# A hybrid decoder block on one core: the loads of branch A's blocks move from SyncE's DMA queue to POOL's

## The chip, the cores and the metric

The kernel runs on one core of one Trainium2 chip. The metric is the device time of one execution in microseconds (us); the time given is the median of several executions. One further execution was recorded by the hardware profiler; its span and its trace are what the rows below come from.

The engines are named as in the profile: PE (TensorE, matmuls), DVE (VectorE), ACT (ScalarE), POOL (GpSimd) and SP (SyncE, which here only issues DMAs). A name with a q behind it (SPq, POOLq) is the engine's sequencer, which issues DMAs and waits for semaphores.

## The reference, cut to what matters

```python
def reference(x, p, w_in, ..., w_branch_a, w_branch_b, w_out, ...):
    h = rms_norm(x, g_pre)
    proj = h @ w_in                                   # 1024 x 1024 @ 1024 x 9216
    u, v, z_a, q, f, inp, z_b, a_a, a_b = split(proj)
    y_a = gmlp_spatial_gating(gelu(u), gelu(v), ...)
    y_a = (y_a * silu(z_a)) @ w_branch_a              # branch A
    o = hgrn2_chunked(q_h, k_in, log_f, v_h)
    o = rms_norm(o, hgrn_norm_g)
    y_b = (o * silu(z_b)) @ w_branch_b                # branch B
    merged = sigmoid(a_a) * y_a + sigmoid(a_b) * y_b
    x = x + rms_norm(merged @ w_out, g_post)
    e = p @ w_ple
    gate = sigmoid(x @ w_ple_gate + b_ple_gate)
    return x + rms_norm(e * gate, g_ple)
```

Sequence and width are 1024, everything is float32. The change lies at the seam between the last columns of `proj` (`a_b`, called AB here) and the product with `w_branch_a`.

## The kernel before

Every large matmul is done with operands split into a high and a low part (`hi`, `lo`): three matmuls stand for one. The split of a tile is a cast on ACT (L134) and a subtraction on DVE (L135). The products of `w_in`, `w_branch_a` and `w_out` are done in two-by-two blocks with seven block products instead of eight (`pair`, whose sums of weight blocks are the tiles `S` and `S2`, made on DVE at L789, and whose results are put together at L812 in tiles `k`, five buffers). A block product is 12 matmuls of 128x512.

The weights of a pair come in two loads of 512 KB with rows of 1 KB (`half_load`, L862). In the main part they land in tiles `raw`; in the stretch looked at here two pairs run in turns (`both`), one with results in the PSUM tiles `big` and one in `small`, and their four loads land in tiles `raw2` (four buffers; the profile prints `raw` for both, the order of instructions keeps them apart by name and number).

What branch A multiplies is computed earlier, block by block, by `mix_a`, and stored to DRAM as seven blocks `af_b11, af_b21, af_b22, af_t1 ... af_t4`. Before the product with `w_branch_a` they are loaded back: the loop at L1002 calls `fill` seven times, `fill` makes two loads of 512 KB each into tiles `raw` (`RAWS` = 3 buffers, rows of 4 KB) and splits them into `a_b11h`, `a_b11l` and so on. These fourteen loads are issued at L891. `fill` is also called at four other places (branch B's blocks, `w_out`, the gate), on which nothing changes here.

The order of instructions on each engine is set by a scheduler when the kernel is built; each engine then runs its own in that order, so an instruction that waits holds everything behind it on that engine. SP issues nearly all loads. POOL issues the stores of intermediate results: `stored` (L905, tiles `k` to `gb_sp` and others), L932 (`bf_sp`) and L766 (`b_sp`, a head's output). Names that the steps below use: `raw2_9424, raw2_9426, raw2_9428, raw2_9430` are the four loads for the pairs AB2 and AB3; `raw2_9753` to `raw2_9769` are the first four of `w_branch_a`; `q<-b_sp7` is the reload (L901) of the last head's output, which POOL stores at L766; `k_9383` is the result at L812 that reads the PSUM bank which the last block product of the projection before AB2 goes on writing.

Of the kernel before, what the change touches and what calls it, by code (L numbers as in the profile page):

```python
# [16 lines left out]
P = 128  # L17
# [16 lines left out]
def hybrid_block(  # L34
# [22 lines left out]
    nc = tc.nc  # L57
    x, p, w_in, out = x[0], p[0, 0], w_in[0], out[0]
# [21 lines left out]
    af_sp = {n: dram.tile([P, 4, 512], F32, name=f"af_{n}") for n in ("b11", "b21", "b22", "t1", "t2", "t3", "t4")}  # L80
# [52 lines left out]
    def split(hi, lo, src):  # L133
        nc.scalar.copy(out=hi, in_=src)  # L134
        nc.vector.tensor_tensor(out=lo, in0=src, in1=hi.bitcast(F32), op=ALU.subtract)  # L135
# [53 lines left out]
    def wide_load(w, kh, c0, pl=None, tag="raw"):  # L189
        raw = (pl or wp).tile([P, 4, 256], F32, tag=tag, name=tag, bufs=RAWS)  # L190
        nc.sync.dma_start(out=raw, in_=w[kh * 512:(kh + 1) * 512, c0:c0 + 256].rearrange("(k p) c -> p k c", p=P))
        return raw
# [21 lines left out]
    def slot(pl, tag, shape, name):  # L214

        return [pl.tile(shape, F32R, tag=f"{tag}{n}", name=f"{name}{n}") for n in "hl"]
# [23 lines left out]
    for tp in range(4):  # L240
        nc.sync.dma_start(out=pins[:, 2 * tp:2 * tp + 2, :],
                          in_=p[tp * 256:(tp + 1) * 256, :].rearrange("(t p) c -> p t c", p=P))
        if tp % 3 == 0:
            s = slice(tp // 3 * 512, tp // 3 * 512 + 512)
            raw = wp.tile([P, 2, 512], F32, tag="raw", name="raw", bufs=RAWS)
# [29 lines left out]
    for quarter in range(4):  # L275
# [5 lines left out]
        if quarter < 2:  # L281
            raw = wide_load(w_in, quarter, COL_I)
# [10 lines left out]
        for kp in range(NK // 2):  # L293
# [4 lines left out]
            for i in range(2):  # L298
                k = 2 * kp + i
                hi, lo = (a(k, q0, 256) for a in hT)  # L300
                src = pt[:, i * 256:(i + 1) * 256]
# [31 lines left out]
    def folded(n, w, name):  # L333

        return kp.tile([P, 4 * n, w], F32, tag=f"{name}m", name=f"{name}m"), kp.tile([P, n, w], F32, tag=f"{name}f", name=f"{name}f")

    def fold(m, f, dst):
# [3 lines left out]
        for k in (2, 3):  # L341
# [3 lines left out]
    m, f = folded(16, 1, "sub")  # L345
    nc.gpsimd.memset(m, 1.0)
    nc.gpsimd.affine_select(out=m, in_=m, pattern=[[-2, 64], [0, 1]], compare_op=ALU.is_equal,
                            fill=0.0, base=0, channel_multiplier=1)
# [6 lines left out]
    for H in (2, 8):  # L355
        ns = 32 // H
        for d in (1, 2, 3):
            m, f = folded(ns // 4, (4 - d) * H, f"q{d}")
# [188 lines left out]
    for g in range(4):  # L547
# [3 lines left out]
                            fill=0.0, base=0, channel_multiplier=-1)  # L551
# [330 lines left out]
    def at(tag):  # L882
        return (xp if tag[0] == "x" else xq), tag

    def fill(tag, src, shape, name):

        b = slot(*at(tag), shape, name)
        n = shape[1] // 2
        for k in (0, n):
            raw = wp.tile([P, n, shape[2]], F32, tag="raw", name="raw", bufs=RAWS)  # L890
            nc.sync.dma_start(out=raw, in_=src[:, k:k + n, :])  # L891
            split(*(a[:, k:k + n, :] for a in b), raw)
        return b

# [105 lines left out]
    a_blocks = {}  # L1000
    wa = loads_of_two(row_parity(w_branch_a), 0)
    for n, tag in (("b11", "x00"), ("t4", "x01"), ("t2", "t1"), ("t1", "t0"), ("t3", "t2"), ("b21", "x10"), ("b22", "x11")):  # L1002
        a_blocks[n] = fill(tag, af_sp[n], [P, 4, 512], f"a_{n}")
        if n in ("t1", "t3"):
            r = next(wa)

# [20 lines left out]

    first = weight_load(cols(w_branch_b, 0, 0))
    B = [fill(tag, bf_sp[k], [P, 2, T], f"B{k}") for k, tag in enumerate(("x00", "x01", "t1", "t0"))]
    wo = row_halves(w_out)  # L1030
    o_blocks = {}
# [4 lines left out]
    for j in range(8):  # L1036
        py = dense_tile()
        w = weight_split(first, split)
        for parts in ((((0, 512),), ((512, 512),)) if j == 7 else (((0, 512), (512, 512)),)):
            accumulate(py, w, (B_part(0), B_part(1)), parts)  # L1040
        if j < 7:
            first = weight_load(cols(w_branch_b, 0, j + 1))
        if j < 3:
            n, tag = (("b11", "t2"), ("t4", "x10"), ("t2", "x11"))[j]
            o_blocks[n] = fill(tag, wo_sp[n] if j else wo[0][:, :, 0:512], [P, 4, 512], f"wo_{n}")
        for half in range(2):
            q = reload(gb_sp[j], half)
            nc.vector.tensor_tensor(out=q, in0=py[half], in1=q, op=ALU.mult)
            nc.vector.tensor_tensor(out=merged(j, half), in0=pairs_of(q), in1=pairs_of(reload(ma_sp[j], half)), op=ALU.add)
# [136 lines left out]
```

## Time and profile before

| | us |
|---|---|
| median of 3 runs | 1241.37 |
| lowest and highest of them | 1239.43, 1244.89 |
| the profiled execution, whole | 1236.92 |
| its span in the trace | 1235.2 |
| PE busy in the span | 1205.0 |
| DVE busy | 875.1 |
| ACT busy | 599.9 |
| POOL busy | 167.6 |

A row of a timeline gives start, duration, engine, line, operation, output<-input, count, and in brackets the idle time of the engine ahead of it with what ended it. In the chain of work that ended last each row is a start, a duration and what the time was spent in. Times are us from the start of the span.

### The profile page before, as it was taken

To read this page: it belongs to the slowest core of one execution; us is meant where nothing else is said; L and a number is where in the kernel's file an instruction comes from. 1 tells how busy PE (TensorE), PEld (TensorE's weight loads), DVE (VectorE), ACT (ScalarE), POOL (GpSimd) and SP (SyncE) were. 2 spreads that over 40 slices of the span, in tenths; PEclk is the share of its full clock that TensorE was granted. 3 is DMA by queue.
4 is the path that set the end of the run, shared out by engine and by line. 5 is a ranking of instruction groups with operands and counts; after the bars stand their busy time and mean duration, and the time that the engine had idled before them with its cause. 6 is when DMAs were issued, how large, how long until landed. Compare 5 with 4: busy or idle time off the path is not lost.

```text
span 1235.2 us, 22089 instructions
## 1 busy us (share of the span) xinstructions
PE 1205.0 (98%) x8536; PEld 1015.4 (82%) x8536; DVE 875.1 (71%) x1747; ACT 599.9 (49%) x1049; POOL 167.6 (14%) x303
## 2 busy tenths in 40 slices
PE   9999999999999999999999999999999999999996
PEld 6999999778887787888878788887788788787886
DVE  5986665567675967687785857756765644988876
ACT  7642433646556456456555545535724321545332
POOL 4136721010100101010101100100110000000000
PEclk9999989999999999999999999999999999999999
DMA  8636622434535446234533433347853874515232
GB/s 302 202 120 222 203 108 95 132 127 136 166 118 170 156 151 211 95 134 149 187 130 111 167 116 120 109 148 235 283 197 129 285 226 145 171 46 177 86 103 69
DMA packets 111978, 192.58 MB, mean 156 GB/s; under 512 B 8920, under 2 KB 68352, under 8 KB 111872
## 3 DMA queue, kind: packets, MB, share of 16 engines
q1 hardware_dynamic: 93904, 132.42, 33.7%
q0 software_dynamic: 17968, 58.74, 13.1%
q8 instruction: 67, 1.10, 0.4%
q14 instruction: 39, 0.32, 0.1%
HBM read 128.48 MB, written 62.65 MB: 155 GB/s over the span
## 4 chain that ended last, share of the span: by engine, by line
PE 54%; issue 25%; DVE 9%; DMA 5%; ACT 3%; POOL 3%; SPq 1%; DVEq 0%; POOLq 0%; ACTq 0%
PE big L785 25%; PE big L169 6%; PE small L785 2%; PE big L206 2%; PE big L207 2%; PE big L205 2%; PE big L1119 2%; PE big L1121 2%; PE big L1120 2%; PE small L109 1%; DMA raw<-in_w_in_dram 1%; DVE lo L135 1%; PE small L206 1%; PE small L207 1%; PE small L205 1%
## 5 line engine op out<-in xcount | busy, mean ns | idle before, releaser
L135 DVE TENSOR_TENSOR lo<-S,hi 128x512 fp32r<-128x512 f32 x168 | 118.0, 705 | 88.1 <-ACT hi L134 87.9
L134 ACT CAST hi<-S 128x512 fp32r<-128x512 f32 x168 | 103.4, 618 | 149.5 <-PE big L785 81.2
L134 ACT CAST hi<-raw 128x512 fp32r<-128x512 f32 x126 | 77.2, 618 | 139.9 <-PE big L785 63.5
L135 DVE TENSOR_TENSOR lo<-raw,hi 128x512 fp32r<-128x512 f32 x126 | 85.7, 687 | 71.5 <-ACT hi L134 69.1
L812 DVE TENSOR_TENSOR k<-big,k 128x512 f32<-128x512 f32 x90 | 61.8, 687 | 16.5 <-PE big L785 12.1
L789 DVE TENSOR_TENSOR S<-raw 128x512 f32<-128x512 f32 x58 | 39.9, 688 | 22.8 <-DMA raw<-in_w_in_dram 19.9
L785 PE MATMUL big<-h11l,hi 128*128 128x512 f32 x108 | 44.4, 411 | 2.3 <-DVE k L812 2.3
L785 PE MATMUL big<-t1l,hi 128*128 128x512 f32 x108 | 43.7, 404 | 2.0 <-ACT hi L134 2.0
L785 PE MATMUL big<-t1h,lo 128*128 128x512 f32 x108 | 43.3, 401 | 1.0 <-DVE lo L135 1.0
L785 PE MATMUL big<-t2l,hi 128*128 128x512 f32 x108 | 43.3, 401 | 0.4 <-ACT k L807 0.4
L785 PE MATMUL big<-t3l,hi 128*128 128x512 f32 x108 | 43.7, 404 | 0.0
L785 PE MATMUL big<-t0l,hi 128*128 128x512 f32 x108 | 43.5, 403 | 0.0
L785 PE MATMUL big<-h00l,hi 128*128 128x512 f32 x108 | 43.3, 401 | 0.0
L785 PE MATMUL big<-h10l,hi 128*128 128x512 f32 x108 | 43.1, 399 | 0.0
L785 PE MATMUL big<-t1h,hi 128*128 128x512 f32 x108 | 43.1, 399 | 0.0
L785 PE MATMUL big<-h11h,lo 128*128 128x512 f32 x108 | 43.0, 398 | 0.0
L785 PE MATMUL big<-h11h,hi 128*128 128x512 f32 x108 | 42.8, 397 | 0.0
L785 PE MATMUL big<-t0h,lo 128*128 128x512 f32 x108 | 42.7, 395 | 0.0
L785 PE MATMUL big<-h10h,lo 128*128 128x512 f32 x108 | 42.6, 394 | 0.0
L785 PE MATMUL big<-t3h,lo 128*128 128x512 f32 x108 | 42.6, 394 | 0.0
L785 PE MATMUL big<-t2h,lo 128*128 128x512 f32 x108 | 42.5, 394 | 0.0
L785 PE MATMUL big<-h00h,lo 128*128 128x512 f32 x108 | 42.5, 393 | 0.0
(670 smaller groups left out, 3834.4 us busy)
## 6 DMA issues: line engine op xcount, KB each, us to landing
raw<-in_w_in_dram SPq DMA_DIRECT2D x66, 512.0 KB, 4.4
xt<-in_x_dram SPq DMA_DIRECT2D x8, 512.0 KB, 7.4
e_sp<-ev SPq DMA_DIRECT2D x8, 512.0 KB, 4.4
v_sp<-tq POOLq DMA_DIRECT2D x32, 128.0 KB, 2.9
wo_t<-t POOLq DMA_DIRECT2D x16, 256.0 KB, 3.5
vn_sp<-tq POOLq DMA_DIRECT2D x16, 256.0 KB, 2.8
q<-vn_sp SPq DMA_DIRECT2D x16, 256.0 KB, 5.9
f_sp<-k POOLq DMA_DIRECT2D x16, 256.0 KB, 2.5
```

What stands on the lines that cost most here:

```text
L134: nc.scalar.copy(out=hi, in_=src)
L135: nc.vector.tensor_tensor(out=lo, in0=src, in1=hi.bitcast(F32), op=ALU.subtract)
L169: nc.tensor.matmul(out=ps[c0 // 512][:, c0 % 512:c0 % 512 + n], lhsT=wt(k), rhs=a(k, c0, n), start=(k == 0 and i == 0), stop=(k == NK - 1 ...
L205: nc.tensor.matmul(out=o, lhsT=al, rhs=hi, start=first, stop=False, **kw)
L206: nc.tensor.matmul(out=o, lhsT=ah, rhs=lo, start=False, stop=False, **kw)
L207: nc.tensor.matmul(out=o, lhsT=ah, rhs=hi, start=False, stop=last, **kw)
L785: nc.tensor.matmul(out=o, lhsT=w[:, k, :], rhs=x_[:, k, :], start=(k == 0 and i == 0 and not onto), stop=(k == 3 and i == 2), skip_group_c ...
L789: nc.vector.tensor_tensor(out=o, in0=x_, in1=y, op=op)
L812: nc.vector.tensor_tensor(out=o, in0=x_, in1=y, op=ALU.add)
L1119: nc.tensor.matmul(out=o, lhsT=parts[:, 1, k, :], rhs=wh, start=(k == 0), stop=False)
L1120: nc.tensor.matmul(out=o, lhsT=parts[:, 0, k, :], rhs=wl, start=False, stop=False)
L1121: nc.tensor.matmul(out=o, lhsT=parts[:, 0, k, :], rhs=wh, start=False, stop=(k == NK - 1))
```

## The change

`fill` gets an argument that names the engine whose queue issues its loads, SyncE's where none is given. The loop of branch A's seven blocks gives POOL's.

```diff
-    def fill(tag, src, shape, name):
+    def fill(tag, src, shape, name, queue=nc.sync):
...
-            nc.sync.dma_start(out=raw, in_=src[:, k:k + n, :])
+            queue.dma_start(out=raw, in_=src[:, k:k + n, :])
...
-        a_blocks[n] = fill(tag, af_sp[n], [P, 4, 512], f"a_{n}")
+        a_blocks[n] = fill(tag, af_sp[n], [P, 4, 512], f"a_{n}", nc.gpsimd)
```

Fourteen DMA issues leave SP and stand on POOL. PE's instructions keep their order. On SP, in the stretch in which the last projections run (`q_9386` is the reload of the last head's output):

```order
 L862 DMA raw_9268<-in_w_in_dram 128x4x256
 L862 DMA raw_9270<-in_w_in_dram 128x4x256
-L891 DMA raw_9715<-af_b11_125 128x1024
-L891 DMA raw_9719<-af_b11_125 128x1024
 L901 DMA q_9386<-b_sp7_76 128x512
 L901 DMA q_9392<-b_sp6_75 128x512
```

Two loads that stood ahead of the reloads, and so ahead of the loads `raw2_9424` to `raw2_9430` that follow them, are gone from SP. On POOL at the same place (the store of the last head's output, then the stores of branch B's last block):

```order
 L766 DMA b_sp7_76<-z_9260 128x1024
 L905 DMA gb_sp2_152<-k_9127 128x512
+L891 DMA raw_9719<-af_b11_125 128x1024
+L891 DMA raw_9725<-af_t4_131 128x1024
 L932 DMA bf_sp3_88<-k_9383 128x512
 L932 DMA bf_sp3_88<-k_9390 128x512
 L932 DMA bf_sp3_88<-k_9364 128x512
 L932 DMA bf_sp3_88<-k_9329 128x512
+L891 DMA raw_9729<-af_t4_131 128x1024
+L891 DMA raw_9735<-af_t2_129 128x1024
```

Two loads now stand behind the store of the head and ahead of four stores, and `raw_9725`, which on SP stood behind all four `raw2` loads, has nothing of SP's ahead of it. On DVE the scheduler writes another order at the start of AB2 and AB3 (`S` are sums of the four `raw2` loads, `lo` the low part of one):

```order
 L789 TENSOR_TENSOR S_9475<-raw2_9424,raw2_9428 128x512
 L789 TENSOR_TENSOR S2_9511<-S_9475,raw2_9424 128x512
+L789 TENSOR_TENSOR S_9493<-raw2_9426,raw2_9430 128x512
+L789 TENSOR_TENSOR S2_9531<-S_9493,raw2_9426 128x512
+L812 TENSOR_TENSOR k_9383<-big_9274,k_9364 128x512
 L135 TENSOR_TENSOR lo_9458<-raw2_9426,hi_9457 128x512
-L812 TENSOR_TENSOR k_9383<-big_9274,k_9364 128x512
-L789 TENSOR_TENSOR S_9493<-raw2_9426,raw2_9430 128x512
 L812 TENSOR_TENSOR k_9364<-big_9273,k_9364 128x512
-L789 TENSOR_TENSOR S2_9531<-S_9493,raw2_9426 128x512
```

`k_9383` stood behind three instructions that need the first three `raw2` loads; it now stands behind four of which one needs the fourth load.

## Rows read from the trace of the kernel before

**Rows 1.** The page: span, and PE's busy time, share of span, instructions.

```profile
span 1235.2 us, 22089 instructions
PE 1205.0 (98%) x8536; PEld 1015.4 (82%) x8536; DVE 875.1 (71%) x1747; ACT 599.9 (49%) x1049; POOL 167.6 (14%) x303
```

**Rows 2.** PE's waits from 790 to 960: total, times, longest (us).

```profile
PE big L785 <- DVE k L812: 2.3, 1, 2.3
PE big L785 <- DVE lo L135: 1.0, 1, 1.0
```

**Rows 3.** The chain that ended last, 824 to 843: start, duration, what.

```profile
825.31 0.34 SPq L891
...
825.70 0.43 SPq L901
...
829.30 9.95 DMA raw<-in_w_in_dram
...
841.28 0.70 DVE k L812
```

**Rows 4.** SP's waits from 780 to 960: total, times, longest (us).

```profile
SPq L891 <- DVE S L789: 18.5, 1, 18.5
...
SPq L891 <- DVE a_t3l L135: 10.6, 2, 8.7
```

**Rows 5.** Timeline of POOL, 740 to 960.

```profile
822.51 0.54 POOL L766 DMA_DIRECT2D b_sp<-z  x1 [0.60 <-ACT z L765]
824.88 0.54 POOL L905 DMA_DIRECT2D gb_sp<-k  x1 [1.83 <-ACT k L921]
844.66 1.74 POOL L932 DMA_DIRECT2D bf_sp<-k  x3 [19.24 <-DVE k L931]
...
889.28 0.54 POOL L905 DMA_DIRECT2D gb_sp<-k  x1 [4.72 <-ACT k L921]
```

**Rows 6.** DMA issues, last us to landing: at 822, at 874, whole span.

```profile
b_sp<-z POOLq DMA_DIRECT2D x1, 512.0 KB, 3.0
...
gb_sp<-k POOLq DMA_DIRECT2D x1, 256.0 KB, 7.0
...
gb_sp<-k POOLq DMA_DIRECT2D x16, 256.0 KB, 2.7
```

**Rows 7.** Timeline of DVE, 829 to 843.

```profile
829.20 0.69 DVE L135 TENSOR_TENSOR lo<-raw,hi 128x512 fp32r<-128x512 f32 x1 [2.06 <-ACT hi L134]
...
839.35 0.69 DVE L789 TENSOR_TENSOR S<-raw,raw 128x512 f32<-128x512 f32 x1 [2.80 <-DMA raw<-in_w_in_dram]
840.07 0.69 DVE L789 TENSOR_TENSOR S<-S,raw 128x512 f32<-128x512 f32 x1
840.68 0.69 DVE L135 TENSOR_TENSOR lo<-raw,hi 128x512 fp32r<-128x512 f32 x1
...
841.88 0.68 DVE L789 TENSOR_TENSOR S<-raw,raw 128x512 f32<-128x512 f32 x1
```

**Rows 8.** Three stretches: length, busy by engine, then PEclk, DMA share, GB/s.

```profile
833.00:835.00 2.00, 2.00 (x11) 1.63 (x10) 0.00 (x0) 0.00 (x0) 0.00 (x0) 1.00 1.09 371
842.00:845.20 3.20, 3.18 (x8) 2.50 (x9) 3.20 (x6) 2.25 (x4) 0.54 (x1) 0.50 0.03 12
217.00:219.00 2.00, 2.00 (x6) 1.49 (x6) 2.00 (x4) 0.94 (x3) 0.00 (x0) 0.57 0.29 87
```

**Rows 9.** The chain that ended last, 863 to 890.

```profile
870.63 6.90 DMA raw<-in_w_branch_a_dram
```

**Rows 10.** Timeline of PE: its stalls at 216, 842 and 886, a product at 900.

```profile
216.79 0.50 PE L785 MATMUL big<-t1l,hi 128*128 128x512 f32 x1 [2.02 <-ACT hi L134]
...
842.02 0.80 PE L785 MATMUL big<-h11l,hi 128*128 128x512 f32 x1 [2.35 <-DVE k L812]
...
886.51 0.50 PE L785 MATMUL big<-a_b11h,lo 128*128 128x512 f32 x1 [1.03 <-DVE lo L135]
...
899.90 0.39 PE L785 MATMUL small<-a_t2l,hi 128*128 128x512 f32 x1
```

## The prediction

> **What bounds the kernel now.** First the busy times [rows 1]: PE is busy in 1205.0 of 1235.2 us, so a change that leaves PE's own work as it is can only give back, or add to, PE's idle time, 30 us over the whole span. The change touches the stretch from the last projections to the end of branch A, so the next view is who made PE wait there [rows 2]: two stalls between 790 and 960, 2.3 us behind a result on DVE (call it stall A) and 1.0 us behind a low part on DVE (stall B). Nothing else in that stretch stops PE. Last, the chain of work at each stall, read backwards.
>
> Stall A [rows 3, 10]: PE goes on at 842.02, after 2.35 us, when DVE has finished `k_9383`, started at 841.28. DVE was late because it runs in order and had stood 2.80 us waiting for a load [rows 7]: the third `raw2` load, in flight for 9.95 us from 829.30. That was issued so late because SP came to it late: SP had waited 18.5 us, its longest wait in the stretch, for a `raw` buffer [rows 4], until a sum on DVE freed it; at 825.31 it issued the second load of `af_b11`, from 825.70 on four reloads, and then the `raw2` loads. At first sight this is what the change cures: that wait is on a load that now leaves SP.
>
> The stall costs more than its length. From 842.0 to 845.2 PE ran at a granted clock of 0.50, the 1.2 GHz level [rows 8], so 3.2 us hold the work of 1.6. Stall A costs 2.35 + 1.6 = 3.95 us. Stall B [rows 9, 10], 1.03 us ahead of 886.51, is the end of an unbroken row of DVE work that begins where a branch A weight load lands (in flight 6.90 us from 870.63); no lower clock follows it. So at most 3.95 + 1.03 = 5.0 us can be gained here, 0.4% of 1236.92.
>
> **The change part by part.** *The issues themselves.* Fourteen issues of 0.34 us [rows 3] leave SP, 4.8 us, and fourteen of 0.54 [rows 5] come to POOL, 7.6 us. Neither is on PE's path: SP waits in this stretch rather than works, and POOL sits idle 19.24 us ahead of its stores of 844.66 [rows 5]. Value 0; if POOL's idle time were gone it would be the 7.6.
>
> *SP's wait.* Behind the two removed loads the next instruction on SP is the reload of the last head's output. It needs POOL's store of that output, issued at 822.51 [rows 5] and landed 3.0 us later [rows 6], at 825.5. The reload went out at 825.70. So one wait of SP takes the place of the other and 0.2 us is gained, not 18. The store itself is not late on POOL: the load put ahead of it is the one that SP had issued before its wait of 18.5 us began, so near 806, long before POOL has a store to issue.
>
> *DVE's new order.* `k_9383` now stands behind two sums of the fourth load instead of one low part. From the starts [rows 7] a sum that follows its own input costs a step of 0.72 us, another instruction one of 0.61. Before: 0.72 + 0.61 + 0.60 = 1.93 from the first sum to `k_9383`; now 0.72 + 0.61 + 0.72 + 0.61 = 2.66. That is +0.7 us on stall A, with nothing to hide it. In addition the fourth load must be there 1.2 us earlier than where DVE used it (at 840.68 instead of 841.88, [rows 7]); the trace only shows that it had landed by 841.88. Bounds 0 and 1.2; I take 0.2, because in the order before its issue was held up behind the landing of a load that is no longer on SP.
>
> *Company on the DMA engines at stall A.* On SP the load `raw_9725` stood behind the four `raw2` loads. On POOL it goes out as soon as its buffer is free, which is after the low part of 829.20 [rows 7], so near 830, while they are in flight. The engines were full then: share 1.09 at 371 GB/s [rows 8]. Its 0.524 MB take 0.524 / 371 = 1.4 us of them. Ends: 0 (POOL's transfer gets only what SP's leaves) and +1.4 (it goes ahead of the third load whole). What the trace shows of a POOL transfer beside full engines is a 256 KB store that took 7.0 us where the median is 2.7 [rows 6]: POOL's side is the one that suffered, so I take half, 0.7. The Trainium skill, page "DMA: Bandwidth & Descriptors", section "Queues, rings and completion order", says that each DMA engine takes its queues in turn, a packet at a time; rows of 4 KB against rows of 1 KB would then put the moved load ahead and the value at +1.4; the 7.0 us store speaks against so good a share for POOL.
>
> Stall A together: −0.2 + 0.7 + 0.2 + 0.7 = +1.4 us; ends −0.2 + 0.7 = +0.5 and −0.2 + 0.7 + 1.2 + 1.4 = +3.1. The clock loss stays as it is, since the stall was already long enough for it.
>
> *Stall B.* The rest of the moved loads wait for a `raw` buffer (DVE's `a_t3l` and its like, [rows 4]), not for SP, so they go out when they did. But the two weight loads of about 870 now share the engines with the next two moved loads, which on SP stood behind them. Ends: the two pass in front whole, 2 x 1.4 = +2.8 us; or the weights, no longer behind an earlier moved load in SP's own queue, land sooner and the 1.03 us vanish. I take +0.5. A stall of 2.02 us was followed by a clock of 0.57 [rows 8, 10] and that of 1.03 by none, so if B passes 2 us some 1.6 us come on top.
>
> *Loads that now stand behind stores.* The last moved load stands behind a store that went out at 889.28 [rows 5]. The store waits for ACT, which before waited there for a moved load itself, so it will go out sooner; even at 889.28, with 0.54 us to issue and 6.90 in flight [rows 9], the load would be there near 897, 3 us ahead of the product at 899.90 [rows 10] that needs what stands behind it on ACT. Value 0; without that cover it would be up to a few us on the second pair of branch A.
>
> Sum against the profiled execution: 1236.92 + 1.4 + 0.5 = 1238.8. That execution was 4.45 us faster than the median of the runs; on the median, 1241.37 + 1.9 = **1243.3 us**.
>
> **The rivals.**
> *SP is set free* (faster). The `raw2` loads land 2.5 us or more sooner and stall A is gone with its clock loss: −3.95, so 1237.4. For it speaks the 18.5 us wait, the largest of SP's. Against it: the reload behind it is bound by a store that POOL issues at 822.51, change or not. It decides from a third load that lands before 837.
>
> *POOL's loads pass SP's weight loads* (slower). Where the engines are full, the loads from POOL's queue go in front. Stall A takes its upper end, +3.1; stall B +2.8 and, being over 2 us, +1.6 of clock: +7.5, so 1248.9. For it: the engines at 371 GB/s with share 1.09. Against it: the store of 7.0 us. It decides from where B passes 2 us.
>
> *Nothing moves.* The moved loads are bound by buffers, the reload by the store, and SP's issue time was never short; DVE's new order is made up by a fourth load that lands sooner and by less queueing at B. 1241.4. The Trainium skill, same page, section "Issuing engines are not separate DMA queues", says that issuing from another engine only saves the sequencer's issue time, here the 4.8 us of SP that lie beside waits: this case. By that sentence the time is unchanged; the trace agrees in that SP's time goes to waits [rows 4], but not in DVE's order, which the sentence does not cover.
>
> **How the numbers follow.** Forecast (+0.5 to +3.5 us) 0.50; nothing moves 0.25; SP set free 0.12; loads pass 0.13. The measurement can tell about 0.5%, 6.2 us, from no change. At most 5.0 us can be gained, so faster by over 0.5% needs the scatter of the runs too (they lie 5.5 us apart): 0.03. Slower by over 0.5% is most of the last rival: 0.10. The rest, 0.87, lies within. The range reaches down to the rival that sets SP free, 1237.5, and up past the one in which the loads pass, 1250: it leaves out about half of the first and the tail of the second.
>
> **What would show it.** The reloads on SP still go out at about 825.5 and the `raw2` loads behind them: if they go out 10 us sooner the store was not what bound them. PE's wait for `k` at L812 is 3 to 4.5 us (2.35 before), with the fourth load ahead of it on DVE; under 2 us means SP was set free. PE's wait for a low part at the start of branch A is 0.5 to 2 us; over 2 us with a clock near 0.5 behind it is the slower rival. The loads at L891 on POOL start within a microsecond of the times at which SP issued them, except the third, about 2 us sooner. The forecast is wrong if PE waits at a new place, above all behind an ACT cast of a moved load.

## The result, and the profile after

The changed kernel took 1244.4 us (median of 20 runs, 1237.14 to 1250.78). The kernel before, run again beside it, took 1237.41 us (median of 20, 1233.6 to 1244.89). The ratio is 1.0052, 95% interval 1.0036 to 1.0068: the change makes the kernel slower by about 6.4 us (0.0052 of 1237.41), at the 0.5% that the prediction called the least it could tell from no change. The two medians lie 7.0 us apart; what follows goes by the ratio.

The forecast was +1.9 us, to 1243.3. So 1244.4 lies beside the number written down, but that is luck, two errors that cancel: the three runs shown of before lay about 4 us above the later median, and the effect came out about 4.5 us larger than forecast. The sign and the places of the loss hold, the size doesn't.

The profiled execution of the change is its longest run (1250.78 us). The head of its page, to be set beside [rows 1]:

```profile
span 1249.1 us, 22099 instructions
PE 1216.8 (97%) x8536; PEld 1026.6 (82%) x8536; DVE 879.7 (70%) x1747; ACT 600.1 (48%) x1049; POOL 172.8 (14%) x317
```

PE has the same 8536 instructions and is busy 11.8 us longer; most of that lies ahead of the changed stretch (see the section on scatter), the rest is about what the lower clock behind the two stalls adds, since matmuls at a lower clock count as busy. PE's waits from 815 to 1000 us (total, times, longest):

```profile
PE big L785 <- DVE k L812: 4.4, 2, 4.1
PE big L785 <- DVE lo L135: 1.5, 1, 1.5
PE big L169 <- DVE B3l L135: 0.7, 1, 0.7
PE big L785 <- ACT hi L134: 0.3, 1, 0.3
```

The same two stalls as in [rows 2], both longer; the second, short wait for `k` and the one at L169 lie past 970 us, behind the stretch. In the timeline of PE (start, length, idle time ahead and what ended it):

```profile
851.43 0.79 PE L785 MATMUL big<-h11l,hi 128*128 128x512 f32 x1 [4.09 <-DVE k L812]
...
895.79 0.50 PE L785 MATMUL big<-a_b11l,hi 128*128 128x512 f32 x1 [0.33 <-ACT hi L134]
...
898.00 0.80 PE L785 MATMUL big<-a_b11h,lo 128*128 128x512 f32 x1 [1.48 <-DVE lo L135]
```

Stall A went from 2.35 [rows 10] to 4.09 us, stall B from 1.03 to 0.33 + 1.48 = 1.81 us.

**Stall A, read backwards.** DVE ahead of it, to be set beside [rows 7]:

```profile
847.96 0.69 DVE L789 TENSOR_TENSOR S<-raw,raw 128x512 f32<-128x512 f32 x1 [1.63 <-DMA raw<-in_w_in_dram]
848.69 0.69 DVE L789 TENSOR_TENSOR S<-S,raw 128x512 f32<-128x512 f32 x1
849.35 0.69 DVE L789 TENSOR_TENSOR S<-raw,raw 128x512 f32<-128x512 f32 x1
850.08 0.69 DVE L789 TENSOR_TENSOR S<-S,raw 128x512 f32<-128x512 f32 x1
850.69 0.68 DVE L812 TENSOR_TENSOR k<-big,k 128x512 f32<-128x512 f32 x1
```

From the first sum to `k_9383` it is now 850.69 - 847.96 = 2.73 us, 1.93 before: DVE's new order costs 0.80. The rest is the load. Two traces are laid over each other at the first product of ZB3, which starts at 823.03 in before and at 830.69 here; PE has no stall from there to stall A. The first sum then comes at 847.96 - 830.69 = 17.27, where it came at 839.35 - 823.03 = 16.32: 0.95 later. 0.95 + 0.80 = 1.75 is the growth of the stall, 4.09 - 2.35 = 1.74.

The DMA issues of this stretch (queue, count, KB each, median us from issue to landing); first before, 825 to 833.8, then the change, 828 to 840:

```profile
raw<-in_w_in_dram SPq DMA_DIRECT2D x4, 512.0 KB, 10.1
raw<-af_t SPq DMA_DIRECT2D x1, 512.0 KB, 9.9
```

```profile
raw<-in_w_in_dram SPq DMA_DIRECT2D x4, 512.0 KB, 9.5
raw<-af_t POOLq DMA_DIRECT2D x1, 512.0 KB, 6.8
```

The first load of `t4` took 9.9 us on SP's queue, behind the four `raw2` loads; on POOL's, issued while they were being issued, it took 6.8 us. It gets through sooner, and the load that DVE waits for comes later. While this load was in flight in the change (837.84 to 844.66) the two queues moved (packets, MB, share of the 16 engines; q1 is SP's queue, q0 POOL's):

```profile
q1 hardware_dynamic: 1600, 1.92, 79.2%
q0 software_dynamic: 177, 0.61, 23.6%
```

POOL's queue got about a quarter of what the engines moved. But the third load needs until near 847.9, so the whole of `t4`'s load was moved before it landed.

**The clock.** One-us windows of the change (busy time by engine, then PEclk, DMA share, GB/s); before had 0.50 for 3.2 us [rows 8]:

```profile
851.43:852.43 1.00, 1.00 (x2) 0.83 (x3) 1.00 (x2) 1.00 (x2) 0.00 (x0) 0.50 0.00 0
...
855.43:856.43 1.00, 1.00 (x4) 0.80 (x3) 0.00 (x0) 0.00 (x0) 0.00 (x0) 0.50 1.01 387
856.43:857.43 1.00, 1.00 (x5) 0.81 (x4) 0.48 (x1) 0.62 (x1) 0.00 (x0) 0.75 0.88 303
...
898.00:899.00 1.00, 1.00 (x2) 0.84 (x3) 1.00 (x2) 1.00 (x3) 0.70 (x2) 0.50 0.90 176
...
901.00:902.00 1.00, 1.00 (x5) 0.78 (x5) 0.48 (x1) 0.94 (x1) 0.25 (x1) 0.84 0.90 225
```

Five windows at 0.50, the 1.2 GHz level, and one at 0.75 follow stall A: 5 x 0.5 + 0.25 = 2.75 us lost, some 2.7 with rounded edges, where before lost 1.6. And stall B, which no lower clock followed before, now has three windows at 0.50 and one at 0.84 behind it, some 1.6 us.

**Stall B.** The chain that ended last has the weight load of [rows 9] again, and ahead of it a moved load:

```profile
871.30 6.37 DMA raw<-af_t
877.67 0.02 issue
877.69 1.06 ACT a_t2h L134
...
881.23 7.72 DMA raw<-in_w_branch_a_dram
```

The weight load is 7.72 us in flight (6.90 before). It is issued 7.91 us after the first `t0` product of AB2, 7.75 before, since its buffer and DVE's row ahead of it hang on the load of `t2`. Two of the moved loads that on SP stood behind it, the second of `t3` and the first of `b21`, go out on POOL while it is in flight:

```profile
882.63 0.53 POOL L891 DMA_DIRECT2D raw<-af_t  x1 [1.81 <-DVE a_t1l L135]
883.99 0.53 POOL L891 DMA_DIRECT2D raw<-af_b  x1 [0.83 <-DVE a_t1l L135]
```

In this pair of traces the change's loss is then: stall A +1.74 and about 1 us of clock, stall B +0.78 and 1.6 of clock, 5.1 in all. Measured over the stretches themselves, which the next section defines (26.12 to 28.90 us at A, 26.04 to 28.61 at B), it is 2.78 + 2.57 = 5.35.

### The profile page after: what moved, and what is told of

Its sections match the earlier page's. It is cut to its first block, busy times and chain, and to the rows that moved or that the text cites. A ratio compares the mean times of both kernels' runs of the same rounds, so it can differ in the third digit from the quotient of the medians.

```text
span 1249.1 us, 22099 instructions
## 1 busy us (share of the span) xinstructions
PE 1216.8 (97%) x8536; PEld 1026.6 (82%) x8536; DVE 879.7 (70%) x1747; ACT 600.1 (48%) x1049; POOL 172.8 (14%) x317
## 4 chain that ended last, share of the span: by engine, by line
issue 45%; PE 39%; POOL 5%; DVE 4%; DMA 3%; ACT 2%; POOLq 0%; DVEq 0%; SPq 0%; ACTq 0%
PE big L785 10%; PE big L169 6%; PE big L207 3%; PE big L206 3%; PE big L205 3%; PE big L1119 2%; PE big L1121 2%; PE big L1120 2%; PE small L785 2%; PE small L207 1%; PE small L206 1%; PE small L205 1%; DMA raw<-bf_sp 1%; PE small L109 1%; DMA raw<-in_w_out_dram 1%
## 5 line engine op out<-in xcount | busy, mean ns | idle before, releaser
L135 DVE TENSOR_TENSOR lo<-S,hi 128x512 fp32r<-128x512 f32 x168 | 122.3, 730 | 91.9 <-ACT hi L134 91.7
L135 DVE TENSOR_TENSOR lo<-raw,hi 128x512 fp32r<-128x512 f32 x126 | 88.7, 712 | 74.9 <-ACT hi L134 72.6
L785 PE MATMUL big<-h10h,hi 128*128 128x512 f32 x108 | 42.6, 394 | 0.0
```

Source lines behind the costliest of these rows:

```text
L785: nc.tensor.matmul(out=o, lhsT=w[:, k, :], rhs=x_[:, k, :], start=(k == 0 and i == 0 and not onto), stop=(k == 3 and i == 2), skip_group_c ...
```

## The experiments

One trace of each kernel gives four numbers beside the ratio: stall A and the length of the stretch around it (length A: from the first product of ZB3, the projection before AB2, to the first product in the bank set `small`, which is AB3's), and the same for B (from AB2's first `t0` product to the first `a_b11` product in `small`, in branch A). The lengths hold the clock's part. All in us; "by traces" is length A - 24.53 plus length B - 25.73, which are the means of the kernels that leave that part as it was (A: before, before again, e3, e5, e6; B: before, before again, e1; with e2, e7 and e9, which also leave B's loads on SP, the mean of B would be 25.9).

| kernel | stall A | length A | stall B | length B | by traces | ratio, interval |
|---|---|---|---|---|---|---|
| before | 2.35 | 26.12 | 1.03 | 26.04 | | |
| before again, e11 | 1.48 | 23.75 | 0.56 | 25.57 | | |
| the change | 4.09 | 28.90 | 1.81 | 28.61 | +7.3 | 1.0052 (1.0036 to 1.0068) |
| the change, e8 | 3.83 | 27.69 | 2.23 | 27.51 | +4.9 | |
| the change, e12 | 3.98 | 29.04 | 2.46 | 29.10 | +7.9 | |
| e1, b11 | 2.72 | 24.97 | 0.57 | 25.57 | +0.3 | 1.0013 (0.9995 to 1.0032) |
| e2, b11 and t4 | 4.26 | 28.96 | 0 | 24.96 | +3.7 | 1.0023 (1.0008 to 1.0039) |
| e3, the other five | 0.99 | 23.26 | 1.98 | 27.26 | +0.3 | 1.0027 (1.0007 to 1.0047) |
| e4, change and weights | 4.13 | 27.96 | 1.89 | 27.17 | +4.9 | 1.0039 (1.0024 to 1.0055) |
| e5, t2 and t1 | 1.04 | 23.29 | 0.94 | 25.94 | -1.0 | 1.0023 (1.0003 to 1.0043) |
| e6, t3, b21, b22 | 2.36 | 26.22 | 1.47 | 26.76 | +2.7 | 1.0021 (1.0003 to 1.0040) |
| e7, b11 and reloads | 4.29 | 29.02 | 1.47 | 26.62 | +5.4 | 1.0047 (1.0021 to 1.0073) |
| e9, sums on POOL | 0 | 21.98 | 1.48 | 26.49 | -1.8 | 0.9988 (0.9971 to 1.0005) |
| e10, change, sums on POOL | 0.71 | 22.97 | 2.06 | 27.35 | +0.1 | 1.0022 (1.0000 to 1.0044) |

The lengths of the two groups do not overlap. Where b11 and t4 are on POOL with DVE's sums left in place (the change, e2, e4) length A is 27.69 to 29.04, in the five traces that leave A alone 23.26 to 26.22. Where t3 and b21 are on POOL (the change, e3, e4, e6, e10) length B is 26.76 to 29.10, in all others 24.96 to 26.62.

### Parts of the change: e1 to e3, e5, e6

Each moves some of the seven blocks and leaves the others on SP; e2, e3, e5 and e6 differ from e1 in the names of the blocks alone.

```diff
-        a_blocks[n] = fill(tag, af_sp[n], [P, 4, 512], f"a_{n}")
+        a_blocks[n] = fill(tag, af_sp[n], [P, 4, 512], f"a_{n}", nc.gpsimd if n == "b11" else nc.sync)
```

**e1, the two loads of b11.**

> Only the two loads of block b11 are issued from POOL, the other twelve from SP as before. DVE has the order of the changed kernel at stall A (four sums ahead of the result that PE waits for), but the first load of t4 stands behind the raw2 loads on SP again, and stall B's loads are as before. Theory (the loss is DVE's order and a load from another queue beside the weights' loads, each followed by a lower clock): stall A about 2.35 + 0.8 = 3.2 us, stall B near 1.0 with no lower clock behind it, so +1 to +2 us, ratio 1.001. Rival 1 (DVE's order does not matter, all of it is the shared engines): stall A 2.3, within 0.5 us of before. Rival 2 (the loss lies outside the stretch, or comes with any change of the program): +6 us with stalls as before.

Measured 1.0013 (0.9995 to 1.0032). DVE in e1:

```profile
840.52 0.69 DVE L789 TENSOR_TENSOR S<-raw,raw 128x512 f32<-128x512 f32 x1 [1.63 <-DMA raw<-in_w_in_dram]
...
843.20 0.68 DVE L812 TENSOR_TENSOR k<-big,k 128x512 f32<-128x512 f32 x1
```

The change's order on DVE (2.68 us from the sum to `k_9383`) without the company of `t4`: ZB3 starts at 824.57, so the sum comes at 15.95, where it lies without the change (14.95 to 16.33 in the five traces that leave A alone). Moving b11 frees SP of its 18.5 us wait and the `raw2` loads gain nothing by it, as the prediction said of the store; what it brings is DVE's order.

**e2, b11 and t4.**

> The four loads of b11 and t4 are issued from POOL, the other ten from SP. Against the kernel with b11 alone this puts the first t4 load beside the raw2 loads on another queue. Theory: stall A as in the changed kernel, about 4.1 us (0.9 over the one with b11 alone), stall B near 1.0 without a lower clock; +2.5 to +3 us in all, ratio 1.002. Rival 1 (order only): stall A about 3.2. Rival 2: +6 us.

Measured 1.0023 (1.0008 to 1.0039). Stall A is that of the whole change, 4.26, and `k_9383` is late by the load too:

```profile
842.25 0.69 DVE L789 TENSOR_TENSOR S<-raw,raw 128x512 f32<-128x512 f32 x1 [1.71 <-DMA raw<-in_w_in_dram]
```

842.25 less the start of ZB3, 824.84, is 17.41: 1.46 later than in e1. That is the price of `t4` beside the `raw2` loads, and it doesn't rest on these two traces: in the five with `t4` on POOL and the sums on DVE the first sum comes 16.97 to 17.41 after ZB3 (17.22 in the mean), in e1 and the five that leave A alone 14.95 to 16.33 (15.67). A's part of the change is all in these two blocks. Stall B is gone here: the second weight load goes out 6.89 us after AB2's first `t0` product, 0.86 sooner than in before; what makes it sooner isn't shown.

**e3, the other five.**

> The four loads of b11 and t4 stay on SP, the other ten go to POOL. DVE's order at stall A is that of the kernel before. Theory: stall A 2.3 us as before; at the start of branch A the stalls sum to about 1.8 us and a lower clock follows, +2 to +3 us in all, ratio 1.002. Rival 1 (stall B in the changed kernel is only the echo of what came late at stall A): stalls near 1.0 and no lower clock, within 0.5 us of before. Rival 2: +6 us.

Measured 1.0027 (1.0007 to 1.0047). Stall A is 0.99, as low as it gets with the order of before, and stall B is that of the whole change, 0.50 + 1.48. The weight load that B ends on:

```profile
869.78 8.99 DMA raw<-in_w_branch_a_dram
```

8.99 us in flight against 6.90. Parts e2 and e3 add up: 0.0023 + 0.0027 = 0.0050, the whole is 0.0052. With intervals of 0.002 to either side that is weak evidence; the halves of e3 below sum to 0.0044.

**e5, t2 and t1,** and **e6, t3, b21 and b22,** split e3 again.

> Only the four loads of t2 and t1 are issued from POOL; every compute engine keeps the order of the kernel before. Theory now (at stall B the weights' loads are delayed by the loads that went out shortly before and after them from another queue: t3's and the first of b21): these four are not beside them, so the second weight load stays at about 7 us of flight, the stalls at the start of branch A at about 1.0, and the time within 1 us of before. Rival (t2's second load from POOL lands later, holds ACT and DVE, and so the issue of the weights): that load lands 0.7 us later, stalls about 1.7 us, +0.7 to +2 us.

> Only the six loads of t3, b21 and b22 are issued from POOL. Theory: the second weight load is in flight 8 to 9 us (6.9 before), the stalls at the start of branch A sum to about 2.1 us, +1 us without and +2.7 us with a lower clock behind them; the median between, ratio 1.001 to 1.0025. Rival (the late t2 load): flight about 7 us, stalls about 1.0, within 1 us of before.

Measured 1.0023 (1.0003 to 1.0043) and 1.0021 (1.0003 to 1.0040). The weight loads, of e5 and of e6:

```profile
873.69 6.91 DMA raw<-in_w_branch_a_dram
```

```profile
867.87 7.93 DMA raw<-in_w_branch_a_dram
```

With `t2` and `t1` on POOL the weight load takes 6.91 us, as before; with `t3`, `b21` and `b22` there it takes 7.93, near the change's 7.72. The loads that run beside it are `t3`'s and the first of `b21`; which of them costs how much wasn't separated. Over all traces in which it could be read the load takes 6.33 to 7.51 us with these loads on SP and 7.41 to 8.99 with them on POOL. The 7.51 are from e7 (below), which leaves all of B's loads on SP:

```profile
873.14 7.51 DMA raw<-in_w_branch_a_dram
```

So stall B can grow without the moved loads too: e7 and e9 have 1.47 and 1.48. For e6 ratio and trace agree (2.6 and 2.7 us). For e5 they don't: its trace shows nothing in this stretch that is longer than the means, and where its 2.8 us (0.4 to 5.3) come from stays open.

### The weight loads on POOL too: e4

If B came of two queues sharing the engines, then the first four `w_branch_a` loads on POOL, in one row with the moved ones, should take it back.

```diff
-    wa = loads_of_two(row_parity(w_branch_a), 0)
+    wa = loads_of_two(row_parity(w_branch_a), 0, nc.gpsimd)
```

(`half_load` and `loads_of_two` hand the queue on to the issue at L862.)

> The changed kernel with the first four loads of branch A's weights issued from POOL as well, so that moved loads and weights stand in one queue again, in the order in which they stood on SP before. Theory (two queues share the engines, and the weights lose by it): the second weight load is in flight about 7 us as before, the stalls at the start of branch A are 1.2 us or less in all with no lower clock; stall A stays at about 4.1; +2.5 to +3.5 us, ratio 1.002 to 1.003. Rival (a load from POOL's queue is slower in itself): flight 8 us or more, stall B 2 us or more, +6 us or more.

Measured 1.0039 (1.0024 to 1.0055), stall B 0.42 + 1.47, no shorter than in the change. The theory that one queue is enough fell. The second weight load is in flight for 7.41 us here, but it goes out 8.39 us after the first `t0` product, where before sent it 7.75 after: on POOL it stands behind the issue of `t3`'s first load, and that waits for DVE's work on `t2`, whose load lands late. Of the 1.15 us by which it lands later than before, counted from that product, 0.64 are the later issue and 0.51 the longer flight.

### The reloads on POOL: e7

The prediction held that the store of the last head and the four reloads behind it on SP bound the `raw2` loads. e7 moves b11 and these four reloads to POOL (`reload` hands the queue on to the issue at L901).

```diff
-            nc.vector.tensor_tensor(out=q, in0=q, in1=reload(b_sp[2 * jp + i], half), op=ALU.mult)
+            nc.vector.tensor_tensor(out=q, in0=q, in1=reload(b_sp[2 * jp + i], half, nc.gpsimd if jp == 3 else nc.sync), op=ALU.mult)
```

> As the kernel with b11 alone on POOL, and the four reloads of the last two heads' outputs (L901) go to POOL too, where they stand behind the store that they need; SP has nothing left ahead of the raw2 loads. Theory (what bounds the raw2 loads is the landing of the last head's store and the 1 MB of reloads behind it, not the load of b11): the raw2 loads go out when the store has landed, 2.4 us sooner than before and with nothing ahead of them in their queue; stall A 0 to 1.5 us and mostly no lower clock; stall B as before; -2 to -4 us, ratio 0.997 to 0.998. Rival (SP's wait for the buffer was the bound, or the engines are simply full there): stall A as in the kernel with b11 alone, near 2.7 us; +1 to +2 us, ratio 1.001.

Measured 1.0047 (1.0021 to 1.0073): slower, where a gain was expected. The chain that ended last in e7:

```profile
822.21 2.99 DMA b_sp<-z
...
826.48 11.75 DMA raw<-in_w_in_dram
```

and its DVE:

```profile
838.45 0.69 DVE L789 TENSOR_TENSOR S<-raw,raw 128x512 f32<-128x512 f32 x1 [8.87 <-DMA raw<-in_w_in_dram]
...
842.92 1.41 DVE L812 TENSOR_TENSOR k<-big,k 128x512 f32<-128x512 f32 x2
```

Taking the reloads off SP did bring the third load's issue forward, to 826.48 (829.30 in before, with ZB3 0.3 us later), but not past 825.2: in the chain the `raw2` loads wait for the same store. The pool that `raw2` is taken from is opened where the heads' pool, with the tile that this store reads, is closed. The load then takes 11.75 us in place of 9.95, beside reloads that now run with it, so only 0.6 of 2.5 us is left (the sum comes 15.72 after the start of ZB3, 16.32 before), and against the mean of the kernels that leave A alone, 15.61, nothing. And the scheduler's order on DVE puts 842.92 - 838.45 = 4.47 us between that sum and `k_9383`, 1.93 before. What the load gained went into the order.

### DVE's order by itself: e9 and e10

If stall A is what stands ahead of `k_9383` on DVE, taking the sums away from there must remove it, in either kernel. The sums `S` and `S2` of AB2 and AB3 go to POOL; e9 is the kernel before with this edit, e10 the change with it.

```diff
-    def combine(x_, y, op, o):
-        nc.vector.tensor_tensor(out=o, in0=x_, in1=y, op=op)
+    def combine(x_, y, op, o, on=nc.vector):
+        on.tensor_tensor(out=o, in0=x_, in1=y, op=op)
...
-        s1 = combine(a21, a22, ALU.add, sum_tile("S"))
+        s1 = combine(a21, a22, ALU.add, sum_tile("S"), on)
...
-        s2 = combine(s1, a11, ALU.subtract, sum_tile("S2"))
+        s2 = combine(s1, a11, ALU.subtract, sum_tile("S2"), on)
...
-    both(projection("AB", 2, r[0]), projection("AB", 3, r[1], **second))
+    both(projection("AB", 2, r[0], on=nc.gpsimd), projection("AB", 3, r[1], on=nc.gpsimd, **second))
```

> The kernel before (all loads on SP) with one edit: the sums S and S2 of the four raw2 loads of AB2 and AB3 are made on POOL, so that on DVE k_9383 stands behind the two low parts of the first two loads only. Theory (stall A is DVE's order: what stands ahead of k_9383 and which load it needs): before, the second load's cast on ACT ran at 836.73 and the copy that k_9383 needs ended at 837.84, so k_9383 can start near 838.1 in place of 841.28; PE, free at 839.67, does not wait. Stall A 2.35 -> 0 and no lower clock: -2.4 to -4 us, ratio 0.997. Rival (the loads as such set A, whatever the order): k_9383 still starts after 840, stall A over 1 us, ratio 0.999 to 1.001. Rival (POOL is too slow: four sums of some 1.5 us each where DVE took 0.7, the stores of the last branch B block 2 us later): a new wait of PE for a sum in the products that follow, ratio 1.000 or over.

> The change with the same edit: the sums S and S2 of the four raw2 loads on POOL, behind the issue of the moved loads there. Theory (in the change stall A is +0.95 us of later loads and +0.8 us of DVE's order, then the clock): k_9383, 850.69 in the change's trace, comes 3 us or more sooner; stall A 4.09 -> 0 to 1 us, no lower clock behind it; stall B as in the change (1.5 to 2.2). Ratio 1.0052 - 0.0035 = 1.002 (0.9995 to 1.003). Rival (what the change costs lies outside A, in B and ahead of the stretch): ratio 1.004 to 1.006 although stall A is gone. Rival (the sums on POOL hold up what stands behind them): PE waits for a sum or a k buffer behind them, ratio over 1.005.

e9: 0.9988 (0.9971 to 1.0005), 1236.75 us against 1238.51. DVE in e9:

```profile
838.82 0.69 DVE L135 TENSOR_TENSOR lo<-raw,hi 128x512 fp32r<-128x512 f32 x1 [0.76 <-ACT hi L134]
839.43 1.41 DVE L812 TENSOR_TENSOR k<-big,k 128x512 f32<-128x512 f32 x2
```

`k_9383` starts 14.97 after ZB3 (expected 15.07), PE doesn't wait, no lower clock follows, and length A is 21.98, 2.55 under the mean of 24.53. PE's only wait from 815 to 1000 is at B:

```profile
PE big L785 <- DVE lo L135: 1.5, 1, 1.5
```

1.48 us, where the two traces of before have 1.03 and 0.56: PE comes to branch A sooner and the weight loads don't, so part of A's gain is given back there. -2.55 + 0.76 = -1.8 us by the traces, -1.5 by the ratio; the interval doesn't exclude no change, so e9 isn't shown to beat the kernel before.

e10: 1.0022 (1.0000 to 1.0044). Of the change's 0.0052, 0.0030 are gone, 3.7 us, with the loads still on POOL. Stall A is 0.71 (4.09 in the change's trace), with no lower clock; stall B is what it was, 0.57 + 1.49. So the change's cost at A passes through DVE's row of sums to PE. What its trace has left is B, 1.6 us over the mean, and A is 1.6 under it; the ratio's 2.7 us are more than that sum.

### Scatter: e8, e11 and e12

The traces differ ahead of the changed stretch: ZB3 starts at 823.03 in before and 7.66 us later in the change, though PE's and DVE's instructions up to there are the same. PE's busy time (second figure after the window) up to that point, before and the change:

```profile
0.00:823.03 823.03, 807.31 (x6756) 689.22 (x6757) 588.89 (x1209) 433.19 (x764) 151.95 (x274) 0.99 0.45 150
0.00:830.69 830.69, 816.24 (x6756) 698.36 (x6757) 593.80 (x1209) 433.33 (x764) 150.17 (x275) 0.99 0.45 148
```

8.9 of the 11.8 us that PE is busy longer lie here, ahead of the change. e8 and e12 are the change again, e11 the kernel before again.

> The changed kernel once more, for a second trace of it. Theory: stall A 4 us or so, third raw2 load used 17.3 us after the last projection's first product began, as in the first trace; the stalls at the start of branch A sum to about 1.8 us. Whether a lower clock follows is open: it did behind a stall of 2.35 and not behind one of 2.72 in two traces. If the 7.7 us by which the first trace was behind already ahead of the changed stretch came from the change, they are here again; if they are scatter, they are not.

> The kernel before, once more, for the scatter of the stretch ahead of the changed one. The first product of ZB3 (its own first, h00) starts at 823.03 us in the trace of before and at 830.69 and 829.93 in the two traces of the change, whose instructions ahead of that are the same. If the 7 us are scatter, this trace may lie anywhere from 820 to 831 and its stall A from 1.0 to 2.8 us; if they belong to the change it lies at 823 plus or minus 2.

> The change, a third trace. If the 7 us ahead of the stretch are scatter, the first product of ZB3 may start anywhere from 820 to 831; if they belong to the change, at 829 to 831. Stall A 3.8 to 4.1 us (the contention with the moved load and DVE's order are in the program), stall B 1.8 to 2.3 us in all; whether a lower clock follows is open.

ZB3 started at 829.93 in e8, 829.14 in e12 and 828.21 in e11; over all traces the starts lie between 820.47 (e6) and 830.69. So a kernel like before can be 5 us late there without any change, and the 7.66 are within the scatter. Most of them come early: PE's 2000th matmul starts at 270.63 in before and at 277.38 in the change, over 500 us ahead of the first moved load, and at 276.02 in e5 and 274.83 in e11. Three traces of the change at the late end are no proof of the contrary; e10 and e4, also with all fourteen loads on POOL, started at 826.30 and 827.47.

PE's waits in e11 (815 to 1000) are the reading that the prediction lacked:

```profile
PE big L785 <- DVE k L812: 1.5, 1, 1.5
PE big L169 <- DVE B3l L135: 0.7, 1, 0.7
PE big L785 <- DVE lo L135: 0.6, 1, 0.6
```

The same kernel, stall A 1.48 with no lower clock behind it. The one trace the sum was made on had a stall at the long end.

## Why the prediction was right in sign and short in size

**Right as written.** SP's wait: the store of the last head landed at 833.16 and the first reload went out at 833.18, 2.49 us after the start of ZB3 (2.67 before); not 18 us but 0.2 were gained. DVE's order: +0.7 forecast, +0.80 measured, and by itself in e1. The lengths to look for: a wait for `k` of 3 to 4.5 (3.83 to 4.09 in three traces), a wait for a low part of 0.5 to 2 (1.5 each time). Issue time and loads behind stores cost nothing that a trace shows. The fourth load, priced at 0.2, cost 0.05 to 0.1: the sum that needs it starts 0.66 us after the sum ahead of it in the change and 0.71 in e2, where the step is 0.61 without a wait.

**One sign of being wrong that did come.** The prediction was to be wrong if PE waits at a new place. It does: 0.33 us behind a cast `hi` on ACT, 0.75 in e8 and 0.97 in e12. The cast is of a weight, not of a moved load, and it is late because ACT's row hangs on the same weight load as stall B, so it is counted there. Nor do all loads on POOL start within a microsecond of SP's times: counted from AB2's first `t0` product, the second load of `b21` goes out at 20.32, 18.93 before; PE doesn't wait for it.

**The step that failed first: company at A.** The sum took +0.7, half of 1.4, on the ground that a POOL store had taken 7.0 us beside full engines [rows 6] and that POOL's side is the one that suffers. The rows say the opposite for a load of 4 KB rows: 6.8 us on POOL where it took 9.9 on SP, and the third `raw2` load later by 0.95 (profiled pair) or 1.46 (e2 against e1). Between the two groups of traces named under e2 it is 1.55 (17.22 against 15.67). The upper end was right, and the store, with rows of 2 KB and towards DRAM, was the wrong row to judge by. The Trainium skill, page "DMA: Bandwidth & Descriptors", section "Queues, rings and completion order", has each DMA engine take its queues in turn, a packet at a time. The trace agrees in that both queues moved data at once, but not in the share that the prediction drew from it: 177 packets of POOL's queue against 1600 of SP's put a quarter of the bytes on POOL's side, and that was enough for the whole load to pass before the third one landed.

**The second: "the clock loss stays as it is".** The lower clock lasted 3.2 us behind stall A in before (1.6 us lost), more than 5 in two traces of the change (some 2.7 lost) and 3.4 in e8. And it isn't a fixed price in the kernel before: of the five traces that leave A alone two lost it (stalls of 2.35 and 2.36), three didn't (0.99, 1.04, 1.48). With the change it came in 3 of 3, and in e2, e4 and e7, whose stalls are as long. From those five traces to the three of the change stall A grew from 1.64 to 3.97 in the mean, +2.3, and length A from 24.53 to 28.54, +4.0, where the sum had +1.4.

**The third: stall B, +0.5 forecast.** The stall grew by 1.4 in the mean (0.72 to 2.17) and length B by 2.7 (25.73 to 28.41): the loads of `t3` and `b21` beside the weight loads (6.90 to 7.72 in flight; e6), a weight load that goes out a little later, and a lower clock in two of three traces. That the clock would only come in from 2 us of stall was read from a single stall of 2.02; it came behind 0.33 + 1.48 and not behind 0.75 + 1.48.

4.0 + 2.7 = 6.7 us by the traces, 6.4 by the ratio. Nearest to that is the rival in which POOL's loads pass SP's weight loads (+7.5: upper end at A, B grown, a clock loss at B), which had 0.13; the forecast had 0.50 with a range of +0.5 to +3.5. The mechanisms were the forecast's, their sizes that rival's.

"Nothing moves" fell by the interval (1.0036 and up). The Trainium skill, same page, section "Issuing engines are not separate DMA queues", says that issuing from another engine only saves issue time. Here the measurement differs: 6.4 us were lost, because a queue is also an order, and the moved loads left theirs. "SP set free" fell by e1 and e7.

**Open.** e5's 2.8 us; e3's ratio, which is 3 us above what its one trace shows, and e10's, which is 2.6 us above its own; what else than the moved loads lengthens stall B (e7, e9); and whether any of the 7 us ahead of the stretch belongs to the change.

## What to carry to other kernels

A load's place in a queue is also its place behind other loads: move it to an idle engine's queue and it takes bandwidth from the transfers it used to follow (here a quarter of it, and 1.55 us of the load that mattered), so look first at what is in flight when its buffer comes free. Before pricing a stall, ask what stands ahead of the releasing instruction on its in-order engine; two extra sums there cost 0.8 us and taking all four away (e9) emptied the stall, though the whole time stayed within its interval. And take a second trace of the same kernel before building a sum on one stall of it.

## What the runs showed of the hardware

The lower clock isn't tied to the length of a stall alone. A wait of 2.72 us in e1 was followed by none:

```profile
843.50:847.50 4.00, 3.56 (x16) 2.94 (x17) 3.89 (x7) 2.88 (x5) 1.41 (x3) 1.00 0.14 46
```

while 2.35 in before was. In e8 the same stall of the change (3.83) was followed by full clock first and by the lower one a microsecond later:

```profile
850.30:851.30 1.00, 0.89 (x4) 0.76 (x5) 1.00 (x3) 0.91 (x2) 0.00 (x0) 1.00 0.00 0
851.30:852.30 1.00, 1.00 (x5) 0.77 (x4) 1.00 (x3) 0.92 (x3) 0.00 (x0) 0.59 0.00 0
...
853.30:854.30 1.00, 1.00 (x4) 0.80 (x3) 0.05 (x1) 0.00 (x0) 0.84 (x2) 0.50 0.80 217
```

The sums of 128x512 took 1.30 to 1.74 us each on POOL in e9 and 0.69 on DVE, and PE waited for none of them.
